# A hybrid attention and mLSTM layer: TensorE's instructions of one stretch are tied to the order of the source

## The chip, the cores and the metric

The kernel runs on one core of a Trainium2 chip. The metric is the device time of one execution in microseconds (us). The kernel before takes 2219.49 us, the median of three runs (2218.13 to 2221.97).

## The reference

One decoder layer over 2048 tokens of width 1024, all in float32. Cut to what matters:

```
h = rmsnorm(x, norm_g); u = h @ w_in                        # 1024 -> 7168
q_a, k_a, v_a, z_a, x_m, o_m, z_m = split(u)
# group A: 8 heads of 128; three causal dilated windows (128,1), (512,4), (2048,16) with ALiBi,
# merged by a softmax over their log-denominators
att = merge(dilated_window_attention(q_a, k_a, v_a, w, d) for (w, d) in patterns) * silu(z_a)
# group B: 4 heads of 256; mLSTM in chunks, a matrix memory C carried from chunk to chunk
xc = silu(causal_conv(x_m)); q_m, k_m, v_m = headwise(xc, xc, x_m); log_i, log_f = gates(q_m, k_m, v_m)
mls = norm(sigmoid(o_m) * mlstm(q_m, k_m, v_m, log_i, log_f)) * silu(z_m)
y = x + concat(att, mls) @ w_out                            # 2048 -> 1024
out = rmsnorm(y, final_g)
```

## The kernel before, in words

Products that need float32 accuracy are made of rounded high and low parts (`split`, L97 to L99: ScalarE makes the high part, VectorE the low one), so one product is three matmuls: high by high, high by low, low by high.

The program has three stages. The first (to about 1240 us of the span) is the input projection (`product`, L349). The last (from about 2027 us) is the half of the output projection that belongs to the attention (`out_mm`, L1188 to L1190). Between them lies the stretch that the change touches. In it three streams of work are written into one another:

- `attention` (L852) is a generator. It goes through 256 units (8 heads, 16 blocks, a local and a strided kind for each), and each step issues three parts that belong to different units: the scores of unit i (`qk`: three matmuls L748 to L750 into `pq`, then VectorE L752 and ScalarE L754), the transposes of the weights of unit i-2 (`flip`: L762, evicted by L765 or L767), and the product with the values of unit i-3 (`pv`: L780, two profile records each). Once a head is done, its statistics are transposed (`head_stats`, L791), go through DRAM and come back as merge weights, which `spread` (L828) copies over the partitions.
- `mlstm` (L916) is a generator as well. Per chunk and pair of heads it issues L962, L970, L982, L985, L997 and, for the normalisation, L1036 on TensorE. It runs beside the units 18 to 180 (L1254 to L1257).
- `early` (L1092) is the mLSTM half of the output projection: for each half n of the output columns, 16 blocks of tokens, and for each block eight steps e of three matmuls (L1142 to L1144) into one accumulator `pu`. A step needs the split weights `we` (one buffer for each e) and the split activations `me` (three buffers, one for each four steps). Weights and activations arrive in raw tiles `wor` (two buffers, which `load_wo`, L1079, shares).

The loop at L1267 sets how `early` stands between the units: 2.6 steps after each unit, and a step that only loads (`yield 0`) ends the unit's share:

```
    for _ in work:
        owed += 2.6 if i < 259 else 2.0
        while owed >= 1.0:
            owed -= 1.0
            if next(extra, 1) == 0:
                owed = 0.0
```

So in the source the eight steps of the first block stand after four successive units as 2, 3, 2 and 1, and at the swap from n = 0 to n = 1 six units stand between the last step of the one half and the first step of the other.

The order of the source is not the order that runs. The tile framework plans the order of each engine's instructions: it follows the program in time by its own costs, and where the next instruction of an engine isn't ready in that plan it takes a later one that is. What it finds becomes the engine's program. `keep_order` (L654 to L661) can tie it: it links each instruction of the named engines to the one before it in the source, by a dependency that orders them in the plan and needs no semaphore. It is called once before (L678), with an empty list of engines (`KO`, L652).

Of the kernel before, what the change touches and what calls it, by code (L numbers as in the profile page):

```python
# [27 lines left out]
def kernel(  # L28
# [18 lines left out]
    nc = tc.nc  # L47
# [49 lines left out]
    def split(hi, lo, raw):  # L97
        nc.scalar.activation(hi, raw, AF.Copy)  # L98
        nc.vector.tensor_tensor(lo, raw, f(hi), ALU.subtract)  # L99
# [503 lines left out]
    def q_load(d, g):  # L603
        nc.sync.dma_start(f(qt)[:, g], q_d[d["h"]][:, g * 512:(g + 1) * 512])
# [11 lines left out]
    def qk_split(d, g):  # L616
        qr = d["qr", g] = by_r[-1]
        c = -1.0 / math.sqrt(128.0)
        hi, lo = qhi[:, g % 2], qt[:, g]
        nc.scalar.activation(hi, f(lo), AF.Copy, scale=c)  # L620
        nc.vector.scalar_tensor_tensor(lo, f(lo), c, f(hi), op0=ALU.mult, op1=ALU.subtract)
        for i, t in enumerate((hi, lo)):
            nc.gpsimd.tensor_copy(residues(qr[:, i, g % 2]), t.rearrange("p (j r) -> p r j", r=4))
        hi, lo = (residues(d[n])[:, :, g * 128:(g + 1) * 128] for n in ("kh", "k"))
        nc.scalar.activation(hi, f(lo), AF.Copy)
        nc.vector.tensor_tensor(lo, f(lo), f(hi), ALU.subtract)
# [27 lines left out]
    def keep_order(start, engines):  # L654
        last = {}
        for ins in nc.cur_bb.bb.instructions[start:]:
            if ins.engine in engines:
                if ins.engine in last:
                    tc.add_manual_dep(ins, last[ins.engine].name, mybir.DependencyInfo(
                        mybir.DependencyClass.NoSync, mybir.DependencyReason.DATA), reason="issue order")  # L660
                last[ins.engine] = ins  # L661
# [41 lines left out]
    def head_tiles(at, d):  # L703
        h = d["h"]
        c0 = (h % 2) * 128
        vd = v_d[h // 2]
        for n, shape, bufs in (("vn", [128, 16, 128], 2), ("vc", [128, 16, 128], 2), ("zs", [128, T], 1)):
            d[n] = at.tile(shape, F32, name=n, bufs=bufs)
        for r in range(4):
            nc.sync.dma_start(d["vn"][32 * r:32 * r + 32],  # L710
                              vd[:, c0:c0 + 128].rearrange("(b j r) d -> r j b d", r=4, j=32)[r])
        for g in range(4):
            nc.sync.dma_start(
                d["vc"][:, g * 4:(g + 1) * 4, :],
                vd[g * 512:(g + 1) * 512, c0:c0 + 128].rearrange("(j r) d -> j r d", r=4))
        nc.sync.dma_start(d["zs"], za_d[h])
        d["st"] = at.tile([128, 64], F32, name="st", bufs=2)
        d["oL"] = at.tile([128, T], F32, name="oL", bufs=2)
        d["oR"] = at.tile([128, T], F32, name="oR", bufs=2)
        return d  # L720
# [37 lines left out]
    def flip(at, d, u, s, n):  # L758
        R, b = u
        pp = pt.tile([128, 512], F32, name="pt")  # L760
        for i in range(n // 128):
            nc.tensor.transpose(pp[:, i * 128:(i + 1) * 128], s[:, i * 128:(i + 1) * 128], ident)  # L762
        p = at.tile([128, 512], F32, name="p", bufs=3)
        if R and n < 384:
            nc.vector.tensor_copy(p[:, :n], pp[:, :n])  # L765
        else:
            nc.scalar.activation(p[:, :n], pp[:, :n], AF.Copy)  # L767
        return p

    def pv(d, u, p, n):  # L770
        R, b = u
        i = b % 4
        if i == 0:
            d["op", R] = pm.tile([128, 512], F32, name="pm")
        op = d["op", R]
        od = op[:, i * 128:(i + 1) * 128]
        m = n // 128
        for j in range(m):
            v = d["vc"][:, j * 4 + i, :] if R else d["vn"][:, b - m + 1 + j, :]
            nc.tensor.matmul(od, v, p[:, j * 128:(j + 1) * 128], start=j == 0, stop=j == m - 1)  # L780
        if i == 3:
            if R:
                nc.scalar.activation(residues(d["oR"])[:, :, (b - 3) * 32:(b + 1) * 32], residues(op), AF.Copy)
            else:
                nc.scalar.activation(d["oL"].rearrange("p (r b j) -> p b r j", r=4, b=16)[:, b - 3:b + 1],
                                     op.rearrange("p (b j r) -> p b r j", b=4, r=4), AF.Copy)
# [65 lines left out]
    def attention(at):  # L852
        qlag, slag = 0, 2
        units = []
        for h in range(AH):
            for b in range(16):
                units += [(h, (0, b)), (h, (1, b))]
        merges = []
        D_ = {}
        S_ = {}  # L860
        P_ = {}
        for i in range(len(units) + 3):
            if i < len(units):
                h, u = units[i]
                if i == 0:
                    by_r.append(at.tile([128, 2, 2, 512], F32R, name="oL", bufs=2))
                    kh = at.tile([128, T], F32R, name="oR", bufs=2)
                    D_[0] = head_tiles(at, first_load)
                    D_[0]["kh"] = kh
                    qk_split(D_[0], 0)  # L870
                S_[i] = qk(at, D_[h], u)
            if 0 <= i - 2 < len(units):
                h, u = units[i - 2]
                s, n = S_[i - 2]
                P_[i - 2] = flip(at, D_[h], u, s, n)
            if i >= 3:
                h, u = units[i - 3]
                pv(D_[h], u, P_.pop(i - 3), S_.pop(i - 3)[1])
            if i < len(units):
                h, (R, b) = units[i]  # L880
                if R and b % 4 == qlag and h + 1 < AH:
                    if b == qlag:
                        D_[h + 1] = k_load(at if h % 2 == 0 else pre, h + 1)
                    if b >= 4:
                        q_load(D_[h + 1], b // 4 - 1)
                if not R and b == qlag and h:
                    q_load(D_[h], 3)
                if R and b == 11 and h + 1 < AH:
                    head_tiles(at, D_[h + 1])
                    D_[h + 1]["kh"] = (at, ax[0])[h % 2].tile([128, T], F32R, name="kh")  # L890
                if R and b % 4 == slag:
                    if b < 12:
                        qk_split(D_[h], b // 4 + 1)
                    elif h + 1 < AH:
                        qk_split(D_[h + 1], 0)
            if i % 32 == 3 and i > 31:
                stats = head_stats(at, D_[i // 32 - 1])
                next(stats)
            if i % 32 == 9 and i > 31:
                next(stats, None)  # L900
            if i % 32 == 4 and i > 31:
                merges.append(head_merge(at, D_[i // 32 - 1]))
            if merges and i % 32 >= 14 and next(merges[0], "end") == "end":
                merges.pop(0)
            yield
        stats = head_stats(at, D_[AH - 1])
        next(stats)
        for _ in range(8):
            yield
        for g in (stats, head_merge(at, D_[AH - 1])):  # L910
            for _ in g:
                yield
            for _ in range(4):
                yield
# [164 lines left out]
    def load_wo(e):  # L1079
        pool, tag, bufs = ((at, "vn", 2), (at, "vc", 2), (ax[0], "kh", 1), (pre, "k", 1),  # L1080
                           (at, "oL", 2), (at, "oR", 2), (at, "vn", 2), (at, "vc", 2))[e]
        t = pool.tile([128, 2, D], F32R, name=tag, bufs=bufs)
        for n in range(2):
            c = slice(n * 512, (n + 1) * 512)
            raw = raw_tile()
            nc.sync.dma_start(raw, w_out[e * 128:(e + 1) * 128, c])
            split(t[:, 0, c], t[:, 1, c], raw)
            yield
        wo[e] = t
# [126 lines left out]
    def out_last(pss, b):  # L1216
# [3 lines left out]
        for n in range(2):  # L1220
# [6 lines left out]
            if n == 0:  # L1227
# [13 lines left out]
    sel = at.tile([8, 4, 128], F32R, name="sel")  # L1241
    nc.vector.tensor_tensor(sel, ident[:8, 0:4, None].to_broadcast([8, 4, 128]),
                            ident[:8, 4:8, None].to_broadcast([8, 4, 128]), ALU.add)
    work = attention(at)
    for i in range(start):
        next(work)
# [20 lines left out]
# [6 lines that stand above are left out]
        if i >= 230 and loads and next(loads[0], "end") == "end":  # L1273
            loads.pop(0)
        i += 1
    loads += [load_wo(e) for e in range(4, 8)]
    raws[1] = True
    fg = [pool.tile([128, 512], F32, name="bl") for pool in (pre, at)]
# [84 lines left out]
```

## Time and profile before

| what | value |
|---|---|
| median of 3 runs | 2219.49 us |
| profiled execution, its own time | 2220.11 us |
| its span | 2217.2 us |
| granted TensorE clock, mean | 0.988 |
| TensorE busy (matmul) | 2126.7 us, 96% |
| TensorE weight loads busy | 1788.0 us, 81% |
| VectorE busy | 1488.1 us, 67% |
| ScalarE busy | 942.8 us, 43% |

The profile shows one execution. A line number is that of the kernel's source. Names are those of tiles with the buffer numbers left out, so that two units can't be told apart by them, but by their order and shape. Matmuls overlap in the records: the distance between two starts says what one costs, not the length of its bar. A bracket at the end of a timeline row gives the engine's idle time ahead of it and what ended it.

### The profile page before, as it was taken

To read this page: it belongs to the slowest core of one execution; us is meant where nothing else is said; L and a number is where in the kernel's file an instruction comes from. 1 tells how busy PE (TensorE), PEld (TensorE's weight loads), DVE (VectorE), ACT (ScalarE), POOL (GpSimd) and SP (SyncE) were. 2 spreads that over 40 slices of the span, in tenths; PEclk is the share of its full clock that TensorE was granted. 3 is DMA by queue.
4 is the path that set the end of the run, shared out by engine and by line. 5 is a ranking of instruction groups with operands and counts; after the bars stand their busy time and mean duration, and the time that the engine had idled before them with its cause. 6 is when DMAs were issued, how large, how long until landed. Compare 5 with 4: busy or idle time off the path is not lost.

```text
span 2217.2 us, 32676 instructions
## 1 busy us (share of the span) xinstructions
PE 2126.7 (96%) x11826; PEld 1788.0 (81%) x11826; DVE 1488.1 (67%) x3050; ACT 942.8 (43%) x1905; POOL 251.8 (11%) x221
## 2 busy tenths in 40 slices
PE   5999999999999999999999999999898999999998
PEld 4777888998878888787779888888887788777886
DVE  8887768556696558576666578868777644643654
ACT  6433333333383223334344555655555645532221
POOL 2200000000000000000000223343342221210000
PEclk9999999999999999999999999999999999999999
DMA  4256343432263333343324677776675664565442
GB/s 154 95 177 190 114 159 115 158 114 101 90 204 133 114 114 105 125 138 115 133 77 160 186 203 208 213 234 188 195 211 178 192 184 157 173 193 176 162 138 86
DMA packets 278896, 341.52 MB, mean 154 GB/s; under 512 B 22224, under 2 KB 194704, under 8 KB 276688
## 3 DMA queue, kind: packets, MB, share of 16 engines
q1 hardware_dynamic: 277872, 338.85, 48.2%
q8 instruction: 93, 1.52, 0.3%
q10 hardware_dynamic: 864, 0.59, 0.1%
q14 instruction: 67, 0.55, 0.1%
HBM read 222.13 MB, written 117.24 MB: 153 GB/s over the span
## 4 chain that ended last, share of the span: by engine, by line
PE 74%; DVE 9%; DMA 8%; issue 5%; ACT 3%; POOL 1%; SPq 0%; ACTq 0%; DVEq 0%; POOLq 0%
PE pb L349 31%; PE pa L349 12%; PE pm L780 3%; PE pu L997 2%; PE pt L762 2%; PE pu L985 2%; DMA wor<-mls_d 2%; DMA wor<-in_w_out 1%; DMA k<-k_d 1%; PE aux L500 1%; PE aux L510 1%; PE pq L748 1%; PE pq L750 1%; PE pq L749 1%; PE pu L982 1%
## 5 line engine op out<-in xcount | busy, mean ns | idle before, releaser
L98 ACT ACTIVATE whi<-ws 128x1024 fp32r<-128x1024 f32 x140 | 148.2, 1059 | 376.5 <-PE pb L349 209.4
L99 DVE TENSOR_TENSOR wlo<-ws,whi 128x1024 fp32r<-128x1024 f32 x140 | 171.8, 1227 | 81.3 <-ACT whi L98 80.4
L139 DVE TENSOR_TENSOR ws<-w,w 128x1024 f32<-128x1024 f32 x140 | 172.1, 1229 | 24.0 <-DMA w<-in_w_in 22.4
L754 ACT ACTIVATE s<-s,st 128x256 f32<-128x256 f32 (+3 forms) x256 | 134.9, 527 | 76.0 <-DVE st L752 68.8
L411 DVE TENSOR_TENSOR o<-pb,o 128x1024 f32<-128x1024 f32 x84 | 102.8, 1224 | 92.9 <-PE pb L349 91.9
L752 DVE CUSTOM_DVE_ANT_0 s<-pq,bl 128x256 f32<-128x256 f32 (+3 forms) x256 | 114.2, 448 | 43.3 <-PE pq L750 32.0
L612 POOL COPY bl<-bl 128x256 f32<-128x256 f32 x8 | 6.4, 796 | 1150.5 <-DMA q<-q_d 1111.3
L767 ACT ACTIVATE p<-pt 128x256 f32<-128x256 f32 (+1 forms) x192 | 81.3, 424 | 105.7 <-PE pt L762 104.6
L762 PE MATMUL pt<-sc,s 128*128 128x128 f32 x568 | 107.7, 279 | 7.1 <-ACT p L767 5.3
L98 ACT ACTIVATE whi<-w 128x1024 fp32r<-128x1024 f32 x56 | 59.2, 1057 | 125.2 <-PE pb L349 118.7
L1142 PE MATMUL pu<-we,me 128*128 128x512 f32 x256 | 106.6, 417 | 5.3 <-ACT me L98 4.4
L411 DVE TENSOR_TENSOR o<-pa,o 128x1024 f32<-128x1024 f32 x56 | 68.4, 1221 | 62.8 <-PE pa L349 62.8
L1143 PE MATMUL pu<-we,me 128*128 128x512 f32 x256 | 102.1, 399 | 2.9 <-DVE me L99 2.9
L1144 PE MATMUL pu<-we,me 128*128 128x512 f32 x256 | 101.2, 395 | 0.0
L780 PE MATMUL pm<-p,vc 128*128 128x128 f32 x640 | 96.3, 281 | 3.3 <-DVE p L765 1.7
L404 ACT ACTIVATE o<-pb 128x1024 f32<-128x1024 f32 x84 | 84.9, 1016 | 15.6 <-DVE o L411 9.8
L780 PEld LDWEIGHTS pm<-p,vc 128*128 128x128 f32 x640 | 84.0, 195 | 7.0 <-ACT p L767 3.5
L99 DVE TENSOR_TENSOR wlo<-w,whi 128x1024 fp32r<-128x1024 f32 x56 | 68.3, 1220 | 27.5 <-ACT whi L98 27.5
L762 PEld LDWEIGHTS pt<-sc,s 128*128 128x128 f32 x568 | 72.7, 143 | 17.3 <-ACT p L767 6.7
L99 DVE TENSOR_TENSOR me<-wor,me 128x512 fp32r<-128x512 f32 x64 | 48.4, 758 | 56.0 <-ACT me L98 55.9
L780 PE MATMUL pm<-p,vn 128*128 128x128 f32 x496 | 78.7, 279 | 5.1 <-ACT p L767 5.1
L997 PE MATMUL pu<-v,kw 128*128 128x257 f32 x240 | 71.6, 401 | 9.4 <-DVE C L1000 4.8
(592 smaller groups left out, 6565.9 us busy)
## 6 DMA issues: line engine op xcount, KB each, us to landing
w<-in_w_in SPq DMA_DIRECT2D x112, 512.0 KB
wor<-mls_d SPq DMA_DIRECT2D x64, 256.0 KB
q_d<-o SPq DMA_DIRECT2D x8, 1024.0 KB
k_d<-o SPq DMA_DIRECT2D x16, 512.0 KB
vm_d<-vm SPq DMA_DIRECT2D x32, 256.0 KB
xc_d<-xc SPq DMA_DIRECT2D x32, 256.0 KB
qm_d<-qm SPq DMA_DIRECT2D x32, 256.0 KB
v_d<-o SPq DMA_DIRECT2D x8, 1024.0 KB
```

The lines of the kernel that those rows point to most:

```text
L98: nc.scalar.activation(hi, raw, AF.Copy)
L99: nc.vector.tensor_tensor(lo, raw, f(hi), ALU.subtract)
L139: eng.tensor_tensor(s, a, b, ALU.add if sign > 0 else ALU.subtract)
L349: nc.tensor.matmul(out, lhsT, rhs, start=start, stop=stop, skip_group_check=True)
L411: nc.vector.tensor_tensor(dst, ps, src, op)
L752: nc.vector.tensor_tensor_reduce(s[:, :n], ps[:, :n], bias, 1.0, 3e38, ALU.add, ALU.min, accum_out=st[:, col:col + 1])
L754: nc.scalar.activation(s[:, :n], s[:, :n], AF.Exp, bias=st[:, col:col + 1], scale=-1.0, accum_out=st[:, 16 + col:17 + col])
L762: nc.tensor.transpose(pp[:, i * 128:(i + 1) * 128], s[:, i * 128:(i + 1) * 128], ident)
L780: nc.tensor.matmul(od, v, p[:, j * 128:(j + 1) * 128], start=j == 0, stop=j == m - 1)
L997: nc.tensor.matmul(u[:, 0:257], kw[:, 2 * i + e, :], v[:, i], start=True, stop=True)
L1142: nc.tensor.matmul(acc, m[:, 0, j], w[:, 0], start=e == 0, stop=False)
L1143: nc.tensor.matmul(acc, m[:, 1, j], w[:, 0], start=False, stop=False)
```

## The change

The position in the instruction list is noted before the first unit of the attention is issued, and after the loop that interleaves units and `early` steps, `keep_order` is called from that position for TensorE alone. What follows the loop (the rest of `early`, the loads, the last stage) is not tied.

```
+    begin2 = len(nc.cur_bb.bb.instructions)
     work = attention(at)
     for i in range(start):
         next(work)
...
         if i >= 230 and loads and next(loads[0], "end") == "end":
             loads.pop(0)
         i += 1
+    keep_order(begin2, (mybir.EngineType.PE,))
     loads += [load_wo(e) for e in range(4, 8)]
```

## Rows read from the trace of the kernel before

**Rows 1.** The page, part 1: busy time of each engine
```profile
PE 2126.7 (96%) x11826; PEld 1788.0 (81%) x11826; DVE 1488.1 (67%) x3050; ACT 942.8 (43%) x1905; POOL 251.8 (11%) x221
```
**Rows 2.** Windows: length, busy us (count) of each engine, clock, DMA share, GB/s
```profile
1225.00:1985.00 760.00, 713.39 (x4402) 619.67 (x4401) 514.55 (x1721) 413.50 (x1176) 216.35 (x193) 0.98 0.65 195
1240.00:1707.00 467.00, 433.67 (x2840) 386.79 (x2839) 356.48 (x1343) 273.90 (x830) 160.56 (x152) 0.97 0.72 211
...
1755.00:1893.00 138.00, 135.66 (x745) 113.72 (x744) 72.25 (x186) 64.99 (x165) 23.92 (x19) 1.00 0.56 169
...
1985.00:2217.00 232.00, 219.33 (x932) 175.38 (x931) 116.53 (x299) 49.82 (x112) 9.91 (x7) 0.98 0.44 145
```
**Rows 3.** Timeline of TensorE, 1737 to 1756: start, us, line, tiles, count
```profile
1741.90 0.37 PE L748 MATMUL pq<-kh,qh 128*128 128x256 f32 x1
...
1744.19 0.50 PE L1143 MATMUL pu<-we,me 128*128 128x512 f32 x1 [1.20 <-DVE me L99]
...
1753.38 0.36 PE L748 MATMUL pq<-kh,qr 128*128 128x256 f32 x1
...
1754.68 0.50 PE L1144 MATMUL pu<-we,me 128*128 128x512 f32 x1
```
**Rows 4.** Tile we, 1700 to 1765: count, ns min/median/max, first and last start
```profile
L98 ACT ACTIVATE we<-wor x8: 615/626/636, 1725.2 to 1753.2; 128x512 fp32r<-128x512 f32 x8
```
**Rows 5.** Timeline of TensorE, 1889 to 1924
```profile
1900.15 0.39 PE L748 MATMUL pq<-kh,qh 128*128 128x256 f32 x1
...
1904.89 0.94 PE L780 MATMUL pm<-p,vc 128*128 128x128 f32 x6 [1.17 <-ACT p L767]
...
1916.38 0.49 PE L1142 MATMUL pu<-we,me 128*128 128x512 f32 x1
```
**Rows 6.** Timeline of ScalarE, 1899 to 1917
```profile
1915.58 0.62 ACT L98 ACTIVATE me<-wor 128x512 fp32r<-128x512 f32 x1
```
**Rows 7.** Tile me, 1893 to 1940: one user, one wait (us, times)
```profile
L1142 PEld LDWEIGHTS pu<-we,me x26: 186/188/192, 1916.4 to 1938.9; 128*128 128x128 f32 x26
...
  DMA wor<-mls_d: 11.7, 5
```
**Rows 8.** Timeline of TensorE, 1972 to 1985
```profile
1974.38 0.39 PE L1144 MATMUL pu<-we,me 128*128 128x512 f32 x1
...
1978.01 0.39 PE L1142 MATMUL pu<-we,me 128*128 128x512 f32 x1
1980.01 0.71 PE L828 MATMUL pt<-wr,sel 8*128 8x512 f32 x2 [1.61 <-DMA wr<-wm_d]
```
**Rows 9.** Timeline of TensorE, 1706 to 1718
```profile
1707.85 0.44 PE L748 MATMUL pq<-kh,qr 128*128 128x384 f32 x1
...
1710.54 1.06 PE L780 MATMUL pm<-p,vn 128*128 128x128 f32 x4
1712.81 0.66 PE L1036 MATMUL pt<-sc,hm 128*128 128x128 f32 x2 [1.21 <-DVE hm L1031]
```
**Rows 10.** Timeline of TensorE, 1264.5 to 1273
```profile
1265.74 0.42 PE L748 MATMUL pq<-oR,oL 128*128 128x384 f32 x1
...
1267.83 0.34 PE L750 MATMUL pq<-oR,oL 128*128 128x384 f32 x1
1269.02 1.13 PE L962 MATMUL pt<-q,xc 128*128 128x128 f32 x8 [0.85 <-DMA xc<-xc_d]
...
1271.75 0.66 PE L970 MATMUL pt<-sc,xc 128*128 128x128 f32 x4 [1.27 <-DVE E L963]
```
**Rows 11.** Windows, short stretches, among them an idle one (columns of rows 2)
```profile
1323.50:1330.30 6.80, 6.11 (x22) 5.44 (x23) 5.65 (x18) 1.48 (x5) 1.42 (x2) 0.50 0.82 213
1457.40:1460.10 2.70, 0.02 (x1) 0.00 (x0) 0.77 (x2) 1.10 (x4) 1.54 (x3) 0.99 0.98 335
1460.10:1463.40 3.30, 3.28 (x16) 3.28 (x17) 1.48 (x3) 2.27 (x7) 3.30 (x3) 0.50 0.57 153
```
**Rows 12.** Groups of TensorE, 1300 to 1707: busy, mean ns, idle before, releasers
```profile
L997 PE MATMUL pu<-v,kw 128*128 128x257 f32 x216 | 64.6, 402 | 9.4 <-DVE C L1000 4.8 <-DVE sm L990 4.6
```

More of the change, by code (lines that the diff above doesn't have):

```diff
@@ L1243 @@
                             ident[:8, 4:8, None].to_broadcast([8, 4, 128]), ALU.add)
+    begin2 = len(nc.cur_bb.bb.instructions)
     work = attention(at)
@@ L1275 @@
         i += 1
+    keep_order(begin2, (mybir.EngineType.PE,))
     loads += [load_wo(e) for e in range(4, 8)]
```

## The prediction

> **What bounds the kernel now.** I read the page first. TensorE is busy 96% of the span, VectorE, the next, 67% [rows 1]: the kernel is a queue of matmuls, and what matters is where that queue stands still. So the second view is the windows. In the whole stretch that the change ties, 1225 to 1985 us, TensorE is idle 760.0 - 713.4 = 46.6 us. Most of it, 467.0 - 433.7 = 33.3 us, lies beside the mLSTM; from 1755 to 1893 only 138.0 - 135.7 = 2.3 us are idle [rows 2]. The third view is TensorE's timeline, held against the order of the source. Most of the stretch already runs as the source has it. The exceptions are of one kind: an instruction whose data are late, and later ones of the source that run before it. The reader should see in rows 3, 5 and 8 to 10 a score, a value product or an `early` step start before a line that the source puts ahead of it.
>
> **The change part by part.** It adds no instruction and no semaphore. It takes away the filling of these waits: every later matmul stands behind the late one, and with it the softmax work (L752, L754, L765, L767) that VectorE and ScalarE would get from it. Where TensorE has no idle time afterwards, work not done in the wait is done later at its full price. So each place costs the work that now runs ahead, at the moment when the late instruction starts, less later idle time that this work can fill.
>
> First block of `early`, 1737 to 1755. By the source, step e = 7 comes after four units. On the chip eight further score triples start from 1741.90 to 1753.38, before the last matmul of e = 7 at 1754.68 [rows 3]. The reason is the loading of w_out through two raw tiles: the eight splits run from 1725.2 to 1753.2 [rows 4]. Of the 12.8 us from 1741.90 to 1754.68, 1.2 us are idle, and eleven `early` matmuls take 2.6 us at 0.23 us each (sixteen starts, 1974.38 to 1978.01, are 0.227 us apart [rows 8]). The rest, 9.0 us, is work that the source has behind e = 7. I take 9.0. Ends: 4 if ScalarE and VectorE, with less to do, split so much sooner; 11 with the rest of the idle time of this window.
>
> The swap to n = 1, 1900 to 1917. By the source six units separate the halves, and the next step belongs before the score at 1900.15. On the chip it starts at 1916.38 [rows 5], as soon as the split of `me` that began at 1915.58 is through [rows 6]. Of the 16.2 us, 1.6 us are idle (three gaps, the longest 1.17 us [rows 5]), and 1.3 us are a flip, a value product and a spread that stand before it in the source as well. So 13.3 us run ahead. With TensorE standing, the loads may come a little faster; but around here ScalarE and VectorE waited 11.7 us in five waits for the raw tile itself [rows 7], and the transfer doesn't depend on TensorE. I take 12.0; ends 9 and 15.
>
> The last head's merge, 1974 to 1980. The first spread (L828) waits for merge weights that come through DRAM at 1980.01, and sixteen `early` matmuls that the source has behind it run first [rows 8]: 16 x 0.227 = 3.6 us. The statistics start this chain, and they move with everything else, so the wait stays. I take 3.6; ends 2 and 4.
>
> The end of the mLSTM, 1707 to 1713. Three score triples and two value products run from 1707.85 on before L1036, which waits for VectorE until 1712.81 [rows 9]: 5.0 us less 1.6 us idle are 3.3 us. Part of that ran at the lower clock and would cost less later: I take 2.3; ends 0 and 3.3.
>
> The start of the mLSTM, 1265 to 1272. 2.4 us, from 1265.74 to the end of the row at 1267.83, run before L962, whose transfer is late; but 1.27 us of idle time behind it then get filled [rows 10]. I take 1.2; ends 0 and 2.4.
>
> All other places from 1240 to 1707. I find some 30 short runs ahead, most of them one score triple. Three triples and a value product take 2.4 us [rows 10], so a triple takes about 0.6 us, and all of them 18; with the first units, whose value products are placed late as well, 20 is the upper end. The lower end is below nothing, 5 us less, if a part of the idle 33.3 us goes. Whether each late line was truly late can't be read from the rows, but TensorE goes on without a gap at most of these places, so a value near nothing is likelier than the sum: I take 3.0.
>
> The clock. Behind an idle stretch of 2.7 us the granted clock stood at 0.50, the lower of its two levels (1.2 instead of 2.4 GHz), for 3.3 us, and elsewhere for 6.8 us [rows 11]. Half of that is lost: 1.7 to 3.4 us each. The new waits at the first block, at the swap (about 14 us in one piece) and at the merge are all longer than these. I take two falls of 1.7: 3.4; ends 0 and 10.
>
> Sum: 9.0 + 12.0 + 3.6 + 2.3 + 1.2 + 3.0 + 3.4 = 34.5 us. The profiled execution took 2220.1 us, its span and 2.9 us around it, and gives 2254.6; it is 0.6 us above the median, so the median should be 2254.0 us.
>
> **The rivals.** No change, because TensorE isn't truly full and catches up. The windows speak for it at first: from 1755 to 1893 the weight loads are busy 113.7 of 138.0 us, 82%, and from 1985 on 175.4 of 232.0 [rows 2]; a fifth of these stretches would swallow all 34.5 us and give 2220. Against it: where `early` matmuls follow one another with nothing missing, a load takes 0.188 us [rows 7] of 0.227 us [rows 8], 83%. The 82% are thus a full engine, not one with a fifth to spare. The Trainium skill says in "Perfetto Trace Analysis", section "Identifying the Most-Contended Engine", that matmul busy time tells little of the distance to the roofline and that LDWEIGHTS busy should be taken; by that rule this rival would hold, and by the two rows it doesn't.
>
> Faster, because what runs ahead is in the way. Scores that run early put their softmax into ScalarE's and VectorE's queues ahead of what TensorE waits for next: the mLSTM's state update (L1000) and denominators (L990), for which L997 stood idle 9.4 us [rows 12], and the splits of w_out. In the order of the source these would come first. If that took away all 9.4 us, and the splits came as early as TensorE needs them, only the merge and the transfers' waits would be left (3.6 + 1.2): 2220 - 9.4 + 4.8 = 2215. It decides at the splits: they must come 9 and 12 us sooner. For it, VectorE and ScalarE are busy beside the mLSTM; against it, the raw tiles are the late thing at the swap [rows 7], and no queue shortens a transfer.
>
> Much slower: nothing is filled later, the sum of the small places is real (20 instead of 3), and the clock falls at four places for 3.4 us: 34.5 + 17 + 10 = 61 us, 2281.
>
> That the tie does nothing is hardly possible here, as rows 3 and 5 show an order that it forbids.
>
> **How the numbers follow.** Forecast (each long wait costs what ran ahead): 0.74, with its own range 2238 to 2270. Much slower: 0.10. No change: 0.08. Faster: 0.08. About 0.2%, 4.4 us, is what a measurement of this kernel can tell from no change. From these: faster 0.08, within 0.2% 0.08, slower 0.74 + 0.10 = 0.84. All terms at their lower ends come to 4 + 9 + 2 + 0 + 0 - 5 + 0 = 10 us, 2230; the range goes on to 2221, so that it takes in the slower edge of the no-change case, and up to 2276 (the swap at 15, the small places at 15, the clock at 10, the rest as taken: 56 us).
>
> **What would show it.** In the changed kernel's trace the `early` steps of the first block stand between the units as 2, 3, 2 and 1, with idle times of TensorE together near 9 us that splits of `we` or `me` end. At the swap one idle time of 10 to 14 us ends with the split of `me`. L828 of the last head comes ahead of sixteen `early` matmuls, behind some 5 us of idle time. Idle time from 1225 to the end of `early` grows by about 30 us, and the low clock follows at least one of these waits. From the last stage on all times are shifted by the same amount. The prediction is wrong if the splits come sooner by most of the wait, if the mLSTM's 33 us of idle time change by more than 10 us either way, or if the last stage ends its own idle time to take the delay back.

## The result and the profile after

The changed kernel takes 2242.42 us (median of 4 runs, 2237.41 to 2246.35), the kernel before 2218.81 us on the same chip (median of 4): a ratio of 1.0102, 95% interval 1.0077 to 1.0128, or 23.6 us more. The profiled execution took 2246.35 us (span 2244.6), 26.2 us more than that of before, and is the slowest of the four.

The page's part 1, answering [rows 1]:

```profile
PE 2132.6 (95%) x11826; PEld 1798.0 (80%) x11826; DVE 1491.0 (66%) x3050; ACT 947.6 (42%) x1905; POOL 251.6 (11%) x221
```

The instructions are the same in number. TensorE's idle time grew from 2217.2 - 2126.7 = 90.5 to 2244.6 - 2132.6 = 112.0 us, its busy time by 5.9 us. Two windows of the changed kernel, the first one that of [rows 2], with their columns:

```profile
1225.00:1985.00 760.00, 694.11 (x4291) 609.91 (x4290) 502.50 (x1690) 411.43 (x1166) 213.21 (x191) 0.95 0.63 188
...
1768.00:1918.00 150.00, 147.95 (x852) 126.83 (x851) 83.98 (x220) 77.22 (x201) 29.73 (x23) 0.99 0.52 163
```

From 1225 to 1985 TensorE now idles 65.9 us instead of 46.6, and gets 111 matmuls less done. Between the first block and the swap (second row) it idles 2.1 us in 150, about as before.

TensorE's timeline at the first block of `early`, answering [rows 3]: the waits that now stand before its steps.

```profile
1754.55 0.50 PE L1142 MATMUL pu<-we,me 128*128 128x512 f32 x1 [2.02 <-ACT me L98]
...
1763.05 0.50 PE L1142 MATMUL pu<-we,me 128*128 128x512 f32 x1 [0.82 <-ACT we L98]
...
1765.90 0.50 PE L1143 MATMUL pu<-we,me 128*128 128x512 f32 x1 [1.14 <-DVE me L99]
```

And the tile `we` there, answering [rows 4]:

```profile
L98 ACT ACTIVATE we<-wor x8: 613/630/632, 1738.8 to 1762.4; 128x512 fp32r<-128x512 f32 x8
```

The eight splits take 23.6 us from first to last, against 28.0 before. That is better than the forecast, which had taken the splits' times as given.

The swap, answering [rows 5] and [rows 6]: first TensorE, then ScalarE.

```profile
1918.27 0.49 PE L828 MATMUL pt<-wr,sel 8*128 8x512 f32 x1
1931.55 0.80 PE L1142 MATMUL pu<-we,me 128*128 128x512 f32 x1 [12.79 <-ACT me L98]
1932.27 0.79 PE L1143 MATMUL pu<-we,me 128*128 128x512 f32 x1
```

```profile
1924.72 0.63 ACT L98 ACTIVATE we<-wor 128x512 fp32r<-128x512 f32 x1 [2.83 <-DMA wor<-in_w_out]
1926.97 0.63 ACT L98 ACTIVATE we<-wor 128x512 fp32r<-128x512 f32 x1 [1.62 <-DMA wor<-in_w_out]
...
1930.87 0.63 ACT L98 ACTIVATE me<-wor 128x512 fp32r<-128x512 f32 x1 [1.16 <-DMA wor<-mls_d]
```

One idle time of 12.79 us ends when `me` is split. ScalarE itself is idle ahead of each of these three splits, until a transfer into `wor` lands.

The last head's merge, answering [rows 8], and the end and start of the mLSTM, answering [rows 9] and [rows 10], on TensorE:

```profile
1270.25 1.13 PE L962 MATMUL pt<-q,xc 128*128 128x128 f32 x8 [1.93 <-DMA xc<-xc_d]
...
1725.58 1.09 PE L1036 MATMUL pt<-sc,hm 128*128 128x128 f32 x4 [4.25 <-DVE hm L1031]
...
2001.48 0.40 PE L1188 MATMUL pm<-vn,qr 128*128 128x512 f32 x1
...
2004.98 0.39 PE L1188 MATMUL pm<-kh,qr 128*128 128x512 f32 x1
2005.68 0.50 PE L828 MATMUL pt<-wr,sel 8*128 8x512 f32 x1 [0.31 <-DMA wr<-wm_d]
```

At the merge sixteen matmuls of the last stage (L1188 to L1190), which nothing ties, fill the wait; only 0.31 us are idle.

TensorE's groups, 1240 to 1735, of the changed kernel (answering [rows 12]):

```profile
L997 PE MATMUL pu<-v,kw 128*128 128x257 f32 x240 | 71.8, 401 | 12.3 <-DVE sm L990 8.1 <-DVE C L1000 3.9
...
L1036 PE MATMUL pt<-sc,hm 128*128 128x128 f32 x128 | 21.0, 290 | 8.1 <-DVE hm L1031 4.9 <-DVE p L765 1.8 <-ACT p L767 1.1
```

and of before in the same window:

```profile
L997 PE MATMUL pu<-v,kw 128*128 128x257 f32 x240 | 71.6, 401 | 9.4 <-DVE C L1000 4.8 <-DVE sm L990 4.6
...
L1036 PE MATMUL pt<-sc,hm 128*128 128x128 f32 x128 | 21.5, 292 | 1.2 <-DVE hm L1031 1.2
```

Where the delay arises. For a place in the source, take the time by which TensorE has executed everything up to there, and subtract the same of before's profiled execution. The table gives how much this difference grows in three parts: from the start to the end of the mLSTM (1720 us in before's trace), over the first block into the middle of `early`'s first half (1823 us), and from there over the swap and the merge to the end. It covers every kernel run whose TensorE instructions stand in before's source order, apart from work added at the swap. Each row is one execution, and every row is held against the same execution of before, on the first chip. On the other chips before itself ran 5.7 to 7.1 us longer, so a row's end isn't the cost of its change; the ratios of the next section, each on one chip, are that.

```
kernel                                  mLSTM  first block  swap, rest  end
changed kernel                           12.8      4.0        10.7     27.5
the same, other chip (after_again)       10.3      2.1         8.3     20.7
before, other chip (before_again)         2.8     -2.7         2.7      2.8
only mLSTM tied (tie_mlstm)              14.1     -3.6         1.8     12.3
only `early` tied (tie_early)             5.4      4.2        11.8     21.4
junk at the swap (tie_fill)              13.0      4.8        10.4     28.2
units at the swap (tie_gap7)             16.6      4.2         2.1     22.9
only `early` tied, units (te_gap7)        3.6      4.3         2.1     10.0
three raw tiles (tie_wor3)               20.3     -0.4        -1.3     18.6
`early` tied, three tiles (te_wor3)       3.4     -2.7        -0.2      0.5
before, three tiles (free_wor3)          -0.8     -3.2        -1.4     -5.4
```

### The profile page after: what moved, and what is told of

Read it like the earlier page. It is cut to its first block, busy times and chain, and to the rows that moved or that the text cites. A ratio compares the mean times of both kernels' runs of the same rounds, so it can differ in the third digit from the quotient of the medians.

```text
span 2244.6 us, 32708 instructions
## 1 busy us (share of the span) xinstructions
PE 2132.6 (95%) x11826; PEld 1798.0 (80%) x11826; DVE 1491.0 (66%) x3050; ACT 947.6 (42%) x1905; POOL 251.6 (11%) x221
## 4 chain that ended last, share of the span: by engine, by line
PE 75%; DVE 10%; DMA 7%; issue 4%; ACT 3%; SPq 1%; POOL 1%; ACTq 0%; DVEq 0%; POOLq 0%
PE pb L349 31%; PE pa L349 12%; PE pm L780 4%; PE pt L762 2%; PE pu L997 2%; PE pu L985 2%; PE pu L1142 1%; PE pu L1143 1%; PE pu L1144 1%; DMA wor<-in_w_out 1%; PE aux L500 1%; PE aux L510 1%; PE pq L748 1%; PE pq L749 1%; DMA k<-k_d 1%
## 5 line engine op out<-in xcount | busy, mean ns | idle before, releaser
L1142 PE MATMUL pu<-we,me 128*128 128x512 f32 x256 | 109.3, 427 | 19.9 <-ACT me L98 19.1
L404 ACT ACTIVATE o<-pb 128x1024 f32<-128x1024 f32 x84 | 85.0, 1017 | 15.6 <-DVE o L411 9.7
L99 DVE TENSOR_TENSOR wlo<-w,whi 128x1024 fp32r<-128x1024 f32 x56 | 68.3, 1220 | 27.5 <-ACT whi L98 27.5
L997 PE MATMUL pu<-v,kw 128*128 128x257 f32 x240 | 71.8, 401 | 12.3 <-DVE sm L990 8.1
```

The costliest lines, as they stand in the source:

```text
L997: nc.tensor.matmul(u[:, 0:257], kw[:, 2 * i + e, :], v[:, i], start=True, stop=True)
L1142: nc.tensor.matmul(acc, m[:, 0, j], w[:, 0], start=e == 0, stop=False)
```

## The experiments

The kernels ran on three further chips, where before's median was 2224.5 to 2225.9 us and its runs lay between 2214.8 and 2232.4; each ratio is to before on the same chip, with its 95% interval. The first four kernels ran on one chip, the two repetitions, `tie_wor3` and `te_gap7` on the second, the others on the third. A figure with a plus sign is the ratio's share of before's median; "under" gives the difference of two medians.

**The two halves of the tie.** One kernel ends the tie ahead of `early`, the other begins it there.

```diff
+    keep_order(begin2, (mybir.EngineType.PE,))
     woB = ctx.enter_context(tc.tile_pool(name="woB", bufs=1))
...
-    keep_order(begin2, (mybir.EngineType.PE,))
     loads += [load_wo(e) for e in range(4, 8)]
```

> The tie ends before the first instruction of early, so only attention beside the mLSTM is in the order of the source. Theory (each wait costs the work that ran ahead of it, place by place): the changed kernel was 13.5 us behind at 1707 us of the kernel before, and nothing of that came back later, so this run is 10 to 14 us slower than before, 2229 to 2233, and at the swap TensorE has no idle time over 2 us. Rival (the mLSTM part is an accident of one execution and only the waits for w_out cost): within 4 us of before.

```diff
-    begin2 = len(nc.cur_bb.bb.instructions)
     work = attention(at)
...
+    begin2 = len(nc.cur_bb.bb.instructions)
     woB = ctx.enter_context(tc.tile_pool(name="woB", bufs=1))
```

> The tie begins where early begins, so only the units beside early are in the order of the source. Theory: first block 4 us and swap 11 us, the merge near nothing, so 13 to 17 us slower than before, 2232 to 2236, with one idle time of 11 to 14 us at the swap; with the run of the mLSTM part it adds up to the 24 to 27 us of the whole change. Rival (the parts don't add up, since a delay of one part gives the loads of the other time to arrive): the first block's wait alone, 4 to 6 us slower.

Measured: `tie_mlstm` 2231.93 us, ratio 1.0025 (1.0012 to 1.0038), +5.6 us; `tie_early` 2235.97 us, ratio 1.0043 (1.0029 to 1.0057), +9.6 us. Both lie between what the theory asked for (10 to 14 and 13 to 17 us) and what its rival did (under 4, and 4 to 6), so neither expectation held. With `early` tied alone its swap shows the wait:

```profile
1926.16 0.80 PE L1142 MATMUL pu<-we,me 128*128 128x512 f32 x1 [10.63 <-ACT me L98]
```

With the mLSTM tied alone there is none at the swap; its delay arises ahead of 1740, and the free order behind it gives 3.6 us back at the first block (table). Both halves cost, and the larger single wait is the swap's.

**Is the swap's wait the cost, or the clock behind it?** One kernel puts 104 junk transposes in front of the swap's first step, more work that nobody needs; the other puts seven more steps of the attention there, work that is needed anyway.

```diff
+                for _ in range(26):
+                    junk = pt.tile([128, 512], F32, name="pt")
+                    for q in range(4):
+                        nc.tensor.transpose(junk[:, q * 128:(q + 1) * 128], ident, ident)
```

> The whole tie, and 104 transposes of a constant that nobody reads, 11.4 us of TensorE, in front of the first matmul behind the swap, where TensorE waits 12.8 us in the changed kernel. It adds work that the computation doesn't need. Theory (a wait costs its length and then the low clock, which stood from 1919.9 to 1937.0 while work came back at 1931.5): the wait is filled, the granted clock stays at 1.00 there, and 5.4 us at half speed, 2.7 us, come back: 2237 to 2242, 2 to 4 us under the changed kernel. Rival (the clock costs nothing that counts there): no gain, 2242 to 2247, or slower where the fill reaches past the wait.

```diff
+                for _ in range(7):
+                    yield 0
```

> The whole tie, but the source itself puts seven more units between the two halves of early, so that its order is about the one that the free plan had found; the steps that no longer fit run behind the loop, untied. Theory (the order of the source at the swap is what costs, not the tie): the idle time of 12.8 us at the swap falls under 3 us and the run is 8 to 12 us faster than the changed kernel, 2230 to 2235. Rival (the wait belongs to the loads and only moves, or the steps put behind the loop cost as much there): within 3 us of the changed kernel, 2240 to 2246.

Measured: `tie_fill` 2244.37 us, ratio 1.0082 (1.0067 to 1.0096), +18.3 us; `tie_gap7` 2236.84 us, ratio 1.0054 (1.0041 to 1.0067), +12.0 us. TensorE's timeline with the junk:

```profile
1921.80 11.85 PE L1177 MATMUL pt<-sc 128*128 128x128 f32 x104
1933.40 0.48 PE L1142 MATMUL pu<-we,me 128*128 128x512 f32 x1
```

and windows of that kernel at the wait and behind it,

```profile
1921.80:1933.40 11.60, 11.54 (x105) 11.30 (x105) 5.47 (x7) 4.06 (x8) 3.53 (x2) 1.00 0.37 122
1933.40:1945.00 11.60, 11.60 (x67) 9.88 (x66) 5.93 (x13) 5.88 (x14) 0.00 (x0) 1.00 0.42 133
```

against the changed kernel's:

```profile
1921.80:1933.40 11.60, 1.85 (x4) 1.23 (x5) 4.27 (x5) 3.01 (x6) 1.08 (x1) 0.50 0.49 137
1933.40:1945.00 11.60, 11.60 (x58) 9.99 (x57) 5.18 (x12) 5.37 (x14) 0.00 (x0) 0.85 0.36 113
```

The junk takes the wait's place for 11.6 us, the granted clock stays at 1.00 instead of 0.50, and the swap costs the same (10.4 and 10.7 us in the table). So the clock is worth little here: the first six matmuls of the swap take 1.48 us (1933.40 to 1934.88) where the changed kernel, at 0.50, takes 3.02 (1931.55 to 1934.57), 1.5 us. This rests on the rows: the whole time with the junk, +18.3 us against +23.6 and +20.7 of the changed kernel's two measurements, with intervals that overlap, can't tell the 2.7 us that the theory expected from the rival's nothing. The wait is the cost, and work that counts takes it away, as expected: with the seven steps the swap begins without one,

```profile
1938.82 0.49 PE L828 MATMUL pt<-wr,sel 8*128 8x512 f32 x1
1939.24 0.50 PE L1142 MATMUL pu<-we,me 128*128 128x512 f32 x1
```

and the table's "swap, rest" falls from 10.7 to 2.1.

**The same two kernels again, on one chip with the next ones.**

> The changed kernel, whole, on the chip where its parts were run. Theory (the parts are waits at different places and add up): 5.6 (mLSTM part tied alone) + 9.6 (output projection's early part tied alone) = 15 us over before, 12 to 18; in its trace one idle of 10 to 13 us ahead of L1142 at the swap of the column halves. Rival (the two parts make each other worse, because a late mLSTM leaves less free work beside the early blocks): 20 to 28 us over before, as on the first chip.

> The kernel before, unchanged, for a second profiled execution. Theory (in the mLSTM stretch, 1240 to 1707, executions of one and the same program drift by 5 us or so, so that a part of the 13.5 us between the two profiled executions there is not the change's): the second execution reaches the early blocks 3 to 8 us later than the first, with the same order of instructions, and has the same time after that. Rival (the drift of 5.4 us in the kernel with only the early part tied came from its changed loads): under 1 us apart at every source position.

Measured: changed 2244.77 us, ratio 1.0093 (1.0075 to 1.0110); before against itself 1.0006 (0.9992 to 1.0020). The whole costs 20.7 us by its ratio, the halves' sum is 15.2. The rival, that the halves make each other worse, is the nearer one, at its lower end; the whole's interval, 16.7 to 24.5 us, still reaches into the theory's 12 to 18. The table suggests how. When only the mLSTM is tied, the free first block takes 3.6 us of its delay back; when both are tied, it adds 2.1 to 4.8 of its own. The second execution of before drifts by 2.8 us at the end of the mLSTM, a little under what the theory asked for, and is level again in the middle of `early`. So single rows of the mLSTM's column are good to some 3 us at best, and the 20.3 of `tie_wor3` lies 6 above the mean of its kind: its profiled execution, 2237.52 us, took 8.3 us more than that kernel's median. Six executions with an untied mLSTM give 2.4 us on average there (with before's own at 0), six with a tied one 14.5.

**Three raw tiles.** The chain load, split, load through `wor` is loosened by a third buffer, in the changed kernel, with `early` tied alone, and in the kernel before. To make room a small tile, `halo`, moves to another pool.

```diff
-        return woB.tile([128, 512], F32, name="wor", bufs=2)
+        return woB.tile([128, 512], F32, name="wor", bufs=3)
...
-            raw["w", n, e] = woB.tile([128, 512], F32, name="wor", bufs=2)
+            raw["w", n, e] = woB.tile([128, 512], F32, name="wor", bufs=3)
...
-            raw["m", n, b, i] = woB.tile([128, 512], F32, name="wor", bufs=2)
+            raw["m", n, b, i] = woB.tile([128, 512], F32, name="wor", bufs=3)
```

> The changed kernel with three raw tiles (wor) in place of two, so that the load of a w_out piece waits for the split two pieces back. Theory (the swap's wait is the chain of load, split, load through two raw tiles): the idle ahead of L1142 at the swap falls from 12.8 us to 4 to 9, the first block's by 1 to 3, and the time is 4 to 9 us under the changed kernel's on this chip. Rival 1 (the loads themselves, not the tiles, set the pace): idle 12 to 13 as before, no gain. Rival 2 (ScalarE and VectorE are late with the splits for other work queued ahead): idle 10 to 13, gain under 2.

> Only the early part tied, with three raw tiles. Theory (first block and swap are the only costs of this part's tie, and both are the chain through two raw tiles): no idle over 3 us ahead of L1142; -3 to +1 us against before, where two raw tiles gave +9.6. Rival (the order itself costs, tiles aside): +4 us or more.

> The kernel before with three raw tiles. Theory (before's planner already puts other work ahead of the blocks that wait for w_out's splits): -2 to +1 us against before. Rival (the loads through two raw tiles hold up something in before too, as its merge at the end): -4 us or more.

Measured: `tie_wor3` 2229.19 us, ratio 1.0022 (1.0006 to 1.0037), 15.6 us under the changed kernel on that chip; `te_wor3` 2218.91 us, ratio 0.9972 (0.9957 to 0.9986), 5.6 us under before; `free_wor3` 2217.10 us, ratio 0.9966 (0.9950 to 0.9982), 7.4 us under before. The swap of `tie_wor3` starts without a wait:

```profile
1928.86 0.79 PE L828 MATMUL pt<-wr,sel 8*128 8x512 f32 x1
1929.58 0.80 PE L1142 MATMUL pu<-we,me 128*128 128x512 f32 x1
```

and the splits of `we` at the swap of `te_wor3` (tile `we`, 1885 to 1945) stand closer,

```profile
L98 ACT ACTIVATE we<-wor x8: 613/628/632, 1886.5 to 1905.6; 128x512 fp32r<-128x512 f32 x8
```

19.1 us against 22.8 in the changed kernel (1904.2 to 1927.0). With three tiles neither first block nor swap costs anything, in the table's every row that has them. So both costs of tying `early` are the chain through two raw tiles, and the gain of 15.6 is about twice what I expected: the swap's wait went whole, where I had left 4 to 9 us of it. What the move of `halo` does by itself was not tested. The rival on `free_wor3` holds as well: the planner had hidden that chain only in part.

**Units at the swap, with `early` tied alone.** The edit is that of `tie_gap7`, on `tie_early`.

> Only the early blocks and their run-ahead streams tied, with seven more steps of the other streams ahead of the swap's first block. Theory (the swap costs because nothing else stands ahead of its first matmul in the source; with work put there the wait is filled): no idle over 3 us at the swap; 9.6 (early part tied) - 9 to 11 (swap) = -1.5 to +2 us against before, the first block's 4 us balanced by nothing or by the merge. Rival (the work put there is missing later, so the wait only moves to the merge at the end of the early part): +7 to +10 us against before, and an idle of 6 us or more behind the swap.

Measured: 2230.15 us, ratio 1.0027 (1.0014 to 1.0041), +6.0 us. The wait at the swap is gone:

```profile
1925.19 0.50 PE L1142 MATMUL pu<-we,me 128*128 128x512 f32 x1
```

But I had subtracted its whole length from the +9.6 and forgotten that the first block's 4.3 us stay; here that wait is a single one:

```profile
1748.02 0.79 PE L1142 MATMUL pu<-we,me 128*128 128x512 f32 x1 [7.03 <-ACT me L98]
```

4.3 + 2.1 = 6.4 us in the table agree with the 6.0 measured. The expected sum was wrong, its rival's idle time behind the swap is half there (3.93 us ahead of L1142 at 2025.44), without a price in "swap, rest".

**Drawing out the last normalization of the mLSTM.** L1036 waits 7.8 to 9.0 us in the six profiled executions with a tied mLSTM. The seven steps of that normalization were given one attention step each. (In `tie_mlstm_tail` the tie also ends ahead of `early`, in `tie_wor3_tail` there are three raw tiles.)

```diff
-    total, done, start, end, lag = 16 * 25, 0, 18, 180, 3
+    total, done, start, end, lag = 16 * 25 - 7, 0, 18, 176, 7
...
-        for _ in side:
-            pass
         for i in range(lag):
+            next(side)
             next(work)
```

> Only the mLSTM stretch tied, and the last chunk's normalization (7 steps, with the transposes of L1036) drawn out: one attention step after each of its steps, where seven of them stood in three attention steps. Theory (half or more of what the tie costs in this stretch is the wait for that normalization, 8 us ahead of L1036 in every tied trace and 1.2 to 2.3 in every untied one, because no other work stands between its steps in the source): the idle ahead of L1036 falls to 1 to 3 us and the time to 0 to +3 us over before, against +5.6 with the tie alone. Rival (the waits ahead of L997 and L962, or the lower clock, make the 5.6): idle ahead of L1036 falls, the time stays at +4 to +7.

> The whole change with three raw tiles and the last normalization drawn out. Theory (the terms add): +4.9 (three raw tiles) - 3 to 6 (normalization) = -1 to +2 us against before. Rival: +3 to +6, as with three raw tiles alone.

Measured: `tie_mlstm_tail` 2244.26 us, ratio 1.0086 (1.0063 to 1.0109); `tie_wor3_tail` 2243.26 us, ratio 1.0079 (1.0061 to 1.0097). Both are slower than without the edit, by 13 us or so, and both expectations fell, with their rivals. TensorE's groups of `tie_mlstm_tail`, 1240 to 1745:

```profile
L997 PE MATMUL pu<-v,kw 128*128 128x257 f32 x240 | 72.4, 401 | 15.8 <-DVE sm L990 7.0 <-DVE C L1000 5.5 <-DVE m L813 2.0
...
L1036 PE MATMUL pt<-sc,hm 128*128 128x128 f32 x128 | 20.1, 280 | 7.5 <-ACT p L767 4.9 <-DVE hm L1031 2.6
```

L1036 waits as long as ever, now mostly for attention's softmax. The edit also runs 393 steps in 158 rounds instead of 400 in 162, so other lines stand side by side all along the mLSTM: up to the last L1036 TensorE idles 53.3 us, against 45.7 in `tie_mlstm`. The experiment doesn't isolate the normalization. It shows that under a tied order a change of the interleaving alone can move the time by 13 us.

The traces show that this wait was the wrong place to look. The table's measure, read at more places of the source, gives the time that each stretch takes, in us:

```
stretch, by before's times      before   five untied       six tied
1241 to 1263, first units         22.2   21.9 to 22.1      24.2 to 24.9
1263 to 1276, mLSTM's start       12.5   12.5 to 14.0      14.9 to 15.8
1276 to 1403                     126.6   125.2 to 127.4    124.4 to 127.2
1403 to 1692                     289.7   288.9 to 294.3    296.4 to 306.9
1692 to 1720, mLSTM's end         27.9   26.8 to 28.0      27.6 to 28.0
```

The end, where L1036 waits longest, costs nothing, as its windows show, before's first and the changed kernel's second:

```profile
1692.30:1720.20 27.90, 24.41 (x141) 20.77 (x140) 20.93 (x73) 13.03 (x41) 7.83 (x6) 0.82 0.44 135
1705.37:1732.97 27.60, 21.55 (x140) 18.94 (x140) 20.14 (x71) 12.69 (x41) 7.62 (x6) 0.88 0.47 136
```

TensorE idles 6.1 us there instead of 3.5, but the same matmuls keep it busy for 2.9 us less, at a mean granted clock of 0.88 instead of 0.82. The cost lies in the first units, the start, and most of all between 1403 and 1692. Which waits make it up there stays open; a version that keeps the pattern was not tried.

## Why the prediction was right, and where it was not

The forecast was 2254.0 us, the result 2242.42, slower as forecast and inside the range; the working mechanism, a wait costs what ran ahead in it, holds for the swap and, with other sizes, elsewhere.

- **The swap**, 12.0 us: idle 12.79 us, and 10.18 us in the second execution (10.7 and 8.3 in the table, with the clock); with the seven steps there, the cost goes. Near in size, and right in reason. That the transfers hardly depend on TensorE is right too: from the first split of `we` to that of `me` it takes 26.7 us, 27.9 before.
- **First block**, 9.0 us with 4 as lower end: 4.0 and 2.1. The step that failed is taking the splits' times as given. With nothing run ahead, their span shrank from 28.0 to 23.6 us, which I had named as the reason for the lower end and then not taken.
- **The merge**, 3.6 us: nothing. L828 waits as forecast, but sixteen matmuls of the last stage, as many as the `early` matmuls that may no longer pass, fill the place. The step had only looked at work inside the tie; what follows it in the source was free to move up.
- **The mLSTM** (start 1.2, end 2.3, small places 3.0, so 6.5 us): undersized. The traces show 12.8 and 10.3 us against 0 and 2.8 of before; TensorE's idle time from 1240 to the last L1036 grew from 35.5 to 45.4 us, and from 36.2 to 47.7 in the second executions, about the 10 us more at which the prediction was to count as wrong. With this part tied alone the table has 14.1 us and the ratio 5.6: on that chip the untied mLSTM of `tie_early` already stood at 5.4, and the free first block gives 3.6 back. The end, 2.3, cost nothing, though idle ahead of L1036 grew from 1.2 to 8.1 us. The start took 2.4 to 3.3 us more than in before instead of 1.2. The step that failed is the small places: I had found 18 us of work ahead there and taken 3.0, since TensorE goes on without a gap at most of them; by the means of the stretches they cost about 10 us, 2.4 in the first units, about 9 from 1403 to 1692 and 1 less between. L997's 9.4 us grew to 12.3, so the faster rival's gain is not there either.
- **The clock**, 3.4 us: about 1.5 us at the swap, as one fall was priced. Elsewhere it can't be told from the drift between executions (below).
- **No change** as a rival: the fully used stretch from 1768 to 1918 has weight loads busy 126.8 of 150 us, 85%, and gave back about 1 us of the 17.8 by which TensorE was behind at 1782 us of before's trace. This again speaks against the rule that I cited from the Trainium skill ("Perfetto Trace Analysis", "Identifying the Most-Contended Engine"), read as a measure of spare room (the page names MFU, the share of the peak arithmetic rate, beside it, which I had left out).
- **Faster**: it decided at splits that come 9 and 12 us sooner. They came about 4 and 1 sooner. With a third raw tile they do come in time, and `te_wor3` is faster than before, though not faster than the free order with three tiles.

That the sum came this near is in part luck, as errors of opposite sign offset each other. Against the 27.5 us of the table's first row the forecast of 34.5 is 5.0 too high at the first block, 4.9 at swap and merge together, 3.4 for the clock, whose cost the table's parts hold already, and 6.3 too low in the mLSTM. The two profiled executions differ by 26.2 us in their own times; the changed kernel's lies 3.9 us above its median and before's 1.3 above its own, which leaves the 23.6.

## What to carry to other kernels

Where a planner fills a wait by letting later work pass, tying the order costs that work's time wherever the engine is full afterwards; read it as what runs ahead of the late instruction, but ask also what untied work can still move up and how far the late chain speeds up with its engines free. A wait of this kind is better removed at its source: here one more raw tile made both costs vanish and sped up the free order too. In a tied kernel the source's interleaving is the schedule: one small change of its pattern cost 13 us here, more than the tie of that part. And an idle time in a trace isn't yet a cost: the longest wait of the tied mLSTM cost nothing between two places of the source.

## What the runs showed of the hardware

The time at the lower granted clock (0.50, 1.2 GHz) differs between executions of one program: between 1235 and 2065 us it sums to 37.5 us in one execution of before and 44.4 in the other, 78.5 and 51.2 us in two of the changed kernel, although the order of the instructions is the same. In the mLSTM (1240 us to the last L1036) the delays of the tied kernels go with it: the execution with 30.7 us at 0.50 is 10.3 us behind, that with 54.6 us 20.3. Whether the clock is the reason was not tested. On the first chip before's four runs lay within 3.9 us (2218.11 to 2221.97), on another twelve lay within 17.6 us (2214.83 to 2232.44); effects under 5 us needed the repeated comparisons.
